# Four tokens per one-hot comparison and 80 candidates per head in the first half of an expert layer

## Chip, cores and metric

The kernel runs on one core of a Trainium2 chip. The metric is the device time of one execution in microseconds (us). Each time below is for the whole program, which is one layer with a token mixer and an expert layer, for 512 tokens of width 2048 in fp32.

## The reference, cut to what matters

The change lies in the expert layer (`peer_ffn`). Each token has 8 heads. Each head scores two sets of 128 sub-keys, takes the 16 best of each, adds them pairwise to 256 candidate sums, and takes the 16 best sums. Each of those names one of 128 x 128 experts, and a softmax over the 16 sums gives the gates.

```python
top_s, top_i = lax.top_k(s, 16)                       # s: [.., 8 heads, 2 halves, 128]
cand_s = (top_s[..., 0, :, None] + top_s[..., 1, None, :]).reshape(B, S, 8, -1)
cand_e = (top_i[..., 0, :, None] * 128 + top_i[..., 1, None, :]).reshape(B, S, 8, -1)
best_s, best_pos = lax.top_k(cand_s, 16)
experts = jnp.take_along_axis(cand_e, best_pos, axis=-1)
gates = softmax(best_s)
act = gelu(einsum('td,tkd->tk', xb, u[experts]))      # u, v: 16384 experts of width 2048
out = einsum('tk,tkd->td', gates * act, v[experts])
```

## The kernel before

The program first runs a token mixer (pooling branch, retention, gates, output projection), then `feed`, `query`, `experts_in` and `experts_out`. The last four are written in a hand-made order: what stands earlier in the code stands earlier in each engine's queue. Every engine works through its queue in that order.

All large matrix products take fp32 data as a high and a low part. `split` (L72 to L74) makes both: ScalarE casts to the high part (L73) and VectorE, or GpSimd where told so, subtracts to get the low part (L74). A weight chunk of 128 x 2048 is converted in two halves of 128 x 1024; `half` hands one out and `convert` makes the next, so that (`converted = 2`) two are kept ready ahead of TensorE. Each half feeds 8 steps of three matrix products (L85 to L87), 24 in all. After each half `tick` runs, which in `experts_in` is `step`, with a counter n from 0 to 255.

`experts_in` computes, for 384 of the tokens, the activation of all 16384 experts (128 blocks of two halves each). After every second half ScalarE applies the gelu to the finished block (L1017, tile `gao`). Beside it, `step` feeds in three side jobs:

- R, `route`: takes the 16 best sums. Per head it adds the 16 x 16 candidates (L837) and runs `top16`: two passes of the 8 largest (L819), two of their positions (L820), one that strikes out the first eight (L822). After the 8 heads it splits positions into row and column (L853, L854), then compares them with 0..15 in 8 steps (L865 to L870) to look up the sub-key numbers. It runs first for the 128 tokens whose experts are gathered, then for three tiles of 128 tokens.
- U, `gathers`: GpSimd issues an indirect DMA for one expert row per token (L929); VectorE multiplies and sums it (L978). Three buffers.
- S, `scatter_gates`: spreads the gates of a tile over a 128 x 128 table per token. For each of 32 groups of four tokens it makes one-hots, multiplies them on TensorE in the next S step (L907), and in the step after that ScalarE copies one part from PSUM (L897) and VectorE adds the other (L898), both into the tile `gsc`. After 16 tokens `gsc` is written to memory (L900). `gsc` has one buffer, so the next copy waits for that write.

The order in `step`: U on even n and on n % 16 == 15; S on odd n once a tile is routed; R on every n until then, later on n % 4 == 1, after S.

The one-hots of one token before: GpSimd compares and scales by the gate's high part (L918), VectorE compares and scales by its low part (L920), ScalarE makes the third with two activations (L922, L923), of which the first takes a per-partition bias. The pool `oh` has 7 buffers, one per token.

From the last two blocks of `query` until the first tile is routed, `low_turns` gives every second low half (L74) to GpSimd. The tables `cos` and `sin` of the mixer lie in a pool that is kept to the end.

Of the kernel before, what the change touches and what calls it, by code (L numbers as in the profile page):

```python
# [17 lines left out]
P = 128  # L18
# [12 lines left out]
POOL_ADA = [1, 1, 1, 1, 2, 2, 2, 2, 2, 2, 0, 0]  # L31
ADA_TURNS = {1: (0,), 2: (1,), 3: (2, 3), 4: (4,), 5: (5,), 6: (6, 7), 7: (8,), 8: (9,), 9: (10, 11), 10: (12,),
             11: (13,), 12: (14,), 13: (15,)}
MAGIC = 12582912.0
TWO_PI = 6.283185307179586476925

# [11 lines left out]
class Mixer:  # L48
# [46 lines left out]

    ahead = 3
    low_engine = None
    low_turns = False
    converted = 1

    def fill(self):
# [12 lines left out]
    def convert(self, eng=None, pair=None):  # L114
        while self.loaded and self.loaded[0][1] is not None:
            self.consume()
        if not self.loaded:
            return
        c = self.loaded[0]
        t, _, s = c  # L120
        h, l = (pair or self.next_pair)()
        if self.low_turns:
            self.low_engine = None if self.low_engine else self.nc.gpsimd
        self.split(t[:, s * 1024:(s + 1) * 1024], h, l, eng or self.low_engine)
        self.ready.append((h, l))
        c[2] += 1
        if c[2] == 2:
            self.loaded.pop(0)
            self.fill()
# [154 lines left out]
    def start(self):  # L284
        nc, a = self.nc, self.a
        stt = nc.vector.scalar_tensor_tensor
        self.cond_scope = ExitStack()
        cp = self.cond_scope.enter_context(self.tc.tile_pool(name="cp", bufs=1))
        with ExitStack() as cs:
            tp = lambda n, b=1: cs.enter_context(self.tc.tile_pool(name=n, bufs=b))  # L290
# [115 lines left out]
    def rotary_tables(self, tmp):  # L406
        nc, a = self.nc, self.a
        ts, stt = nc.vector.tensor_scalar, nc.vector.scalar_tensor_tensor
        self.cos = self.const.tile([P, T], FT, name="cos")
        self.sin = self.const.tile([P, T], FT, name="sin")  # L410
        invf = self.const.tile([P, 1], FT, name="invf")
        nc.gpsimd.dma_start(out=invf, in_=a["inv_freq"])
        pos = tmp.tile([P, T], I32, name="sq")
        nc.gpsimd.dma_start(out=pos, in_=a["positions"].to_broadcast([P, T]))
        yield
        c = _pieces(TWO_PI, (4, 11, 18))
        kk = _pieces(float(65536 - 10430 * np.longdouble("6.283185307179586476925286766559")), (4, 11, 18))
        r, h, n = self.sin, self.cos, tmp.tile([P, T], FT, name="rot", bufs=1)
        ts(out=r, in0=pos, scalar1=1.0, scalar2=None, op0=OP.mult)
        yield  # L420
        ts(out=r, in0=r, scalar1=invf, scalar2=None, op0=OP.mult)
        yield
        ts(out=h, in0=r, scalar1=1.0 / 65536, scalar2=MAGIC, op0=OP.mult, op1=OP.add)
        yield
        ts(out=h, in0=h, scalar1=MAGIC, scalar2=None, op0=OP.subtract)
        yield
        stt(out=r, in0=h, scalar=-65536.0, in1=r, op0=OP.mult, op1=OP.add)
        yield
        stt(out=n, in0=h, scalar=sum(kk), in1=r, op0=OP.mult, op1=OP.add)
        yield  # L430
        ts(out=n, in0=n, scalar1=1.0 / TWO_PI, scalar2=MAGIC, op0=OP.mult, op1=OP.add)
        yield
        ts(out=n, in0=n, scalar1=MAGIC, scalar2=None, op0=OP.subtract)
        yield
        for i in range(4):
            stt(out=r, in0=h, scalar=kk[i], in1=r, op0=OP.mult, op1=OP.add)
            yield
            stt(out=r, in0=n, scalar=-c[i], in1=r, op0=OP.mult, op1=OP.add)
            yield
        ts(out=n, in0=r, scalar1=1.0 / TWO_PI, scalar2=MAGIC, op0=OP.mult, op1=OP.add)  # L440
        yield
        ts(out=n, in0=n, scalar1=MAGIC, scalar2=None, op0=OP.subtract)
        yield
        for v in (c[0] + c[1], c[2] + c[3]):
            stt(out=r, in0=n, scalar=-v, in1=r, op0=OP.mult, op1=OP.add)
            yield
        lim = float(np.nextafter(np.float32(np.pi), np.float32(0)))
        ts(out=r, in0=r, scalar1=lim, scalar2=-lim, op0=OP.min, op1=OP.max)
        yield
        nc.scalar.activation(out=h, in_=r, func=AF.Abs)  # L450
        ts(out=h, in0=h, scalar1=-1.0, scalar2=float(np.pi / 2), op0=OP.mult, op1=OP.add)
        yield
        nc.scalar.activation(out=self.cos, in_=h, func=AF.Sin)
        nc.scalar.activation(out=self.sin, in_=r, func=AF.Sin)
# [110 lines left out]
    def retention(self):  # L565
        nc, a = self.nc, self.a
        self.ret = self.dram.tile([32, P, T], FT, name="ret")
        with ExitStack() as cs:
# [76 lines left out]
                pend = finish  # L645
            self.first_gate = self.gemm_t(self.hn)
            pend()

    def load_pairs(self, src, pool):
        out = []  # L650
# [91 lines left out]
    def query(self):  # L742
# [7 lines left out]
        with ExitStack() as cs:  # L750
# [35 lines left out]
            for j in range(KT):  # L786
                b = first[j] if j < 2 else self.gemm_t(self.fn)
                keep(j, b)
                natural(j)
                if j >= KT - 2:  # L790
                    self.low_turns = True
            self.flush()
        self.extra_scope.close()

# [29 lines left out]
    def route(self, t, pool):  # L824
# [6 lines left out]
        bp = mk([P, H, 16], U32, "bp")  # L831
        v4 = self.tv[t].rearrange("p (h s) r -> p h s r", s=2)
        for h in range(H):
            cand = mk([P, 16, 16], FT, "cand")
            x = v4[:, h, 0, :].unsqueeze(2).broadcast_to([P, 16, 16])
            y = v4[:, h, 1, :].unsqueeze(1).broadcast_to([P, 16, 16])
            tt(out=cand, in0=x, in1=y, op=OP.add)  # L837
            c = cand.rearrange("p a b -> p (a b)")
            self.top16(c, c, bv[:, h, :], bp[:, h, :])
            yield  # L840
        nc.vector.tensor_copy(out=tf, in_=self.ti[t])
# [7 lines left out]
        res = []  # L849
        hi = mk([P, H * 16], U32, "hi")  # L850
        lo = mk([P, H * 16], U32, "lo")
        bpf = bp.rearrange("p h k -> p (h k)")
        nc.vector.tensor_scalar(out=hi, in0=bpf, scalar1=4, scalar2=None, op0=OP.logical_shift_right)  # L853
        nc.vector.tensor_scalar(out=lo, in0=bpf, scalar1=15, scalar2=None, op0=OP.bitwise_and)  # L854
        yield
        f4 = tf.rearrange("p (h s) r -> p h s r", s=2)
        for side, pos in ((0, hi), (1, lo)):
            pf = mk([P, H, 16], FT, f"pf{side}")
            nc.vector.tensor_copy(out=pf.rearrange("p h k -> p (h k)"), in_=pos)
            ix = mk([P, H, 16], FT, f"ix{side}")  # L860
            for q in range(4):
                hs = slice(2 * q, 2 * q + 2)
# [13 lines left out]
    def scatter_gates(self, t, i1, i2, gate, tp, oh, gp):  # L876
# [2 lines left out]
        for i, x in enumerate((i1, i2, gate)):  # L879
            nc.tensor.transpose(out=b[:, i * P:(i + 1) * P], in_=x, identity=self.ident)  # L880
        yield
        tr = tp.tile([P, 4, P], FT, name="tr")
        gh = tp.tile([P, P], FR, name="gh")
        gl = tp.tile([P, P], FT, name="gl")
        nc.scalar.copy(out=tr[:, 0:3, :].rearrange("p a b -> p (a b)"), in_=b[:, 0:3 * P])
        self.split(tr[:, 2, :], gh, gl)
        nc.vector.tensor_scalar(out=tr[:, 3, :], in0=tr[:, 1, :], scalar1=-1.0, scalar2=None, op0=OP.mult)
        yield
        made, summed, gs = [], [], None
        for q in range(P // 4 + 2):  # L890
            for bank, n in summed:
                r = n * 2 % GC
# [6 lines left out]
                if r + 2 == GC:  # L899
                    nc.sync.dma_start(out=self.gd[t * (P // GC) + n * 2 // GC], in_=gs.rearrange("p i t -> p (i t)"))  # L900
            summed = []
            for v in (0, 1):
                if made:
                    bank = self.bank()
                    for u in (0, 1):
                        y, x = made[v * 2 + u]
                        nc.tensor.matmul(bank[:, u * 2 * P:(u + 1) * 2 * P], y, x.rearrange("p h i -> p (h i)"),  # L907
                                         start=True, stop=True)
                    summed.append((bank, 2 * (q - 1) + v))
            made = []  # L910
            if q < P // 4:
                for u in range(4):
                    n = q * 4 + u
                    x = oh.tile([P, 2, P], FR, name="ohx")
                    y = oh.tile([P, P], FR, name="ohy")
                    d = oh.tile([P, P], FT, name="ohd", bufs=2)
                    s = slice(n, n + 1)
                    nc.gpsimd.tensor_scalar(out=x[:, 0, :], in0=self.iota, scalar1=tr[:, 0, s], scalar2=gh[:, s].bitcast(FT),  # L918
                                            op0=OP.is_equal, op1=OP.mult)
                    nc.vector.tensor_scalar(out=x[:, 1, :], in0=self.iota, scalar1=tr[:, 0, s], scalar2=gl[:, s],  # L920
                                            op0=OP.is_equal, op1=OP.mult)
                    nc.scalar.activation(out=d, in_=self.iota, func=AF.Abs, bias=tr[:, 3, s], scale=1.0)  # L922
                    nc.scalar.activation(out=y, in_=d, func=AF.Relu, bias=1.0, scale=-1.0)  # L923
                    made.append((y, x))
            yield

    def gather(self, src, pool, name, k):
# [5 lines left out]
    def experts_in(self):  # L933
# [5 lines left out]
        with ExitStack() as left:  # L939
# [1 line left out]
            lp = lambda n, b=1: left.enter_context(tc.tile_pool(name=n, bufs=b, reuse_waits="tile"))  # L941
            rp_ = lambda n, b=1: right.enter_context(tc.tile_pool(name=n, bufs=b, reuse_waits="tile", side="right"))
            ap, up, gg = lp("ap", 2), lp("up", 3), lp("gg")
            rp, trp, oh, gp = rp_("rp"), rp_("trp"), rp_("oh", 7), rp_("gp")
            act = gg.tile([P, P], FT, name="act")
            gate = gg.tile([P, P], FT, name="ggate")
            fnat = gg.tile([P, D], FT, name="fnat")
# [41 lines left out]
            def step():  # L989
                n = count[0]  # L990
                count[0] += 1
                if scattering:
                    self.low_turns, self.low_engine = False, None
                odd, e = n % 2, n // 2
                if not routed or not scattering:
                    next(R, None)
# [319 lines left out]
```

## Time and profile before

| | |
|---|---|
| median of 3 runs | 4974.7 us (4973.16 to 4975.7) |
| profiled execution, its own time | 4985.34 us |
| span of its instructions | 4983.6 us, 58696 instructions |
| mean granted clock of TensorE | 0.988 of full speed |
| busy: TensorE, weight load, VectorE, ScalarE, GpSimd | 4832.4, 4173.4, 3237.4, 1704.9, 1570.5 us |
| `experts_in`, by its gelu (L1017) | from 2752.8 to 3903.5 us |

The busy times are of one profiled execution. Matrix products are pipelined, so each is shown longer than the step from one to the next; the count of products per microsecond tells better how fast TensorE goes. PE is TensorE, PEld its weight loads, DVE is VectorE, ACT is ScalarE, POOL is GpSimd, SP is the queue that issues most DMAs. An arrow in a row reads "output from inputs".

### The profile page before, as it was taken

To read this page: it belongs to the slowest core of one execution; us is meant where nothing else is said; L and a number is where in the kernel's file an instruction comes from. 1 tells how busy PE (TensorE), PEld (TensorE's weight loads), DVE (VectorE), ACT (ScalarE), POOL (GpSimd) and SP (SyncE) were. 2 spreads that over 40 slices of the span, in tenths; PEclk is the share of its full clock that TensorE was granted. 3 is DMA by queue.
4 is the path that set the end of the run, shared out by engine and by line. 5 is a ranking of instruction groups with operands and counts; after the bars stand their busy time and mean duration, and the time that the engine had idled before them with its cause. 6 is when DMAs were issued, how large, how long until landed. Compare 5 with 4: busy or idle time off the path is not lost.

```text
span 4983.6 us, 58696 instructions
## 1 busy us (share of the span) xinstructions
PE 4832.4 (97%) x22905; PEld 4173.4 (84%) x22905; DVE 3237.4 (65%) x4296; ACT 1704.9 (34%) x2703; POOL 1570.5 (32%) x1125
## 2 busy tenths in 40 slices
PE   6889999999999999999989999999999999999998
PEld 5668888888888888888878999999999888888887
DVE  8873334434332245655567998888787688888876
ACT  3332222222222222222232346556566433332233
POOL 6440000000000010000010367777788344444433
PEclk9999999999999999999999999999999999999999
DMA  6442222222233356765732577887888989898884
GB/s 265 178 148 87 102 102 99 95 102 95 92 126 131 125 190 227 263 228 204 237 107 99 172 275 282 291 295 275 308 294 314 327 310 326 317 332 323 316 284 152
DMA packets 268454, 1058.12 MB, mean 212 GB/s; under 512 B 22656, under 2 KB 73904, under 8 KB 173328
## 3 DMA queue, kind: packets, MB, share of 16 engines
q1 hardware_dynamic: 208960, 726.71, 42.2%
q0 software_dynamic: 54416, 325.48, 17.2%
q8 instruction: 181, 2.97, 0.2%
q10 hardware_dynamic: 4800, 2.16, 0.2%
q14 instruction: 97, 0.79, 0.0%
HBM read 973.53 MB, written 80.75 MB: 212 GB/s over the span
## 4 chain that ended last, share of the span: by engine, by line
PE 72%; DVE 11%; issue 8%; DMA 5%; POOL 2%; ACT 2%; SPq 0%; POOLq 0%; DVEq 0%; ACTq 0%
PE bank L87 24%; PE bank L85 24%; PE bank L86 24%; DVE wlc L74 2%; DVE urow L978 1%; DVE rawc L188 1%; DMA gd<-gsc 1%; DMA rawc<-in_w_ada_dram 1%; POOL ohx L918 1%; DVE u L513 1%; DMA x<-m 1%; ACT whc L73 1%; PE bank L907 1%; DVE gsc L898 0%; DVE eq L869 0%
## 5 line engine op out<-in xcount | busy, mean ns | idle before, releaser
L74 DVE TENSOR_TENSOR wlc<-rawc,whc 128x1024 fp32r<-128x1024 f32 x905 | 1158.3, 1286 | 993.5 <-ACT whc L73 992.9
L73 ACT CAST whc<-rawc 128x1024 fp32r<-128x1024 f32 x968 | 998.9, 1050 | 1995.4 <-PE bank L86 1093.8
L85 PE MATMUL bank<-act,whc 128*128 128x512 f32 x2816 | 1101.8, 391 | 27.8 <-ACT act L347 19.0
L86 PE MATMUL bank<-act,whc 128*128 128x512 f32 x2816 | 1102.8, 392 | 24.1 <-DVE act L356 20.2
L87 PE MATMUL bank<-act,wlc 128*128 128x512 f32 x2816 | 1102.1, 391 | 6.4 <-POOL wlc L74 3.6
L87 PE MATMUL bank<-fh,wlc 128*128 128x384 f32 (+1 forms) x2304 | 792.7, 344 | 15.6 <-DVE wlc L74 12.9
L85 PE MATMUL bank<-fh,whc 128*128 128x384 f32 (+1 forms) x2304 | 793.3, 344 | 4.8 <-ACT whc L73 2.8
L86 PE MATMUL bank<-fl,whc 128*128 128x384 f32 (+1 forms) x2304 | 791.1, 343 | 0.7 <-DVE fl L734 0.5
L86 PEld LDWEIGHTS bank<-act,whc 128*128 128x128 f32 x2816 | 531.8, 189 | 141.0 <-DVE act L356 24.8
L85 PEld LDWEIGHTS bank<-act,whc 128*128 128x128 f32 x2816 | 532.1, 189 | 138.8 <-ACT act L347 19.0
L87 PEld LDWEIGHTS bank<-act,wlc 128*128 128x128 f32 x2816 | 531.8, 189 | 120.3 <-POOL wlc L74 4.9
L918 POOL TENSOR_SCALAR ohx<-iota,tr,gh 128x128 fp32r<-128x128 f32 x384 | 586.9, 1535 | 75.1 <-PE bank L907 70.7
L85 PE MATMUL bank<-whc,ph 128*128 128x512 f32 x1536 | 602.7, 392 | 1.0 <-ACT ph L73 1.0
L87 PE MATMUL bank<-whc,pl 128*128 128x512 f32 x1536 | 600.5, 391 | 0.0
L86 PE MATMUL bank<-wlc,ph 128*128 128x512 f32 x1536 | 597.7, 389 | 1.6 <-DVE wlc L74 1.6
L87 PEld LDWEIGHTS bank<-fh,wlc 128*128 128x128 f32 x2304 | 436.0, 189 | 30.3 <-DVE wlc L74 16.1
L85 PEld LDWEIGHTS bank<-fh,whc 128*128 128x128 f32 x2304 | 436.5, 189 | 15.7 <-ACT whc L73 4.0
L86 PEld LDWEIGHTS bank<-fl,whc 128*128 128x128 f32 x2304 | 436.0, 189 | 11.3 <-DVE fl L734 2.0
L929 POOL DMA_INDIRECT vrow<-in_v_dram,eidx x128 | 273.7, 2138 | 488.4 <-DVE accg L1076 473.2
L188 DVE SCALAR_TENSOR_TENSOR rawc<-rawc,cond 128x2048 f32<-128x2048 f32 x96 | 241.8, 2520 | 198.7 <-DMA rawc<-in_w_ada_dram 198.7
L86 PEld LDWEIGHTS bank<-wlc,ph 128*128 128x128 f32 x1536 | 288.4, 188 | 65.0 <-DVE wlc L74 2.4
L87 PEld LDWEIGHTS bank<-whc,pl 128*128 128x128 f32 x1536 | 288.2, 188 | 64.8 <-DVE pl L74 0.3
(285 smaller groups left out, 5292.9 us busy)
## 6 DMA issues: line engine op xcount, KB each, us to landing
rawc<-in_ut_dram SPq DMA_DIRECT2D x128, 1024.0 KB, 5.7
rawc<-in_v_dram SPq DMA_DIRECT2D x128, 1024.0 KB, 7.5
rawc<-in_w_ada_dram SPq DMA_DIRECT2D x96, 1024.0 KB, 5.3
rawc<-in_w_v_dram SPq DMA_DIRECT2D x32, 1024.0 KB, 4.9
rawc<-in_w_g_dram SPq DMA_DIRECT2D x32, 1024.0 KB, 4.8
rawc<-in_w_br_dram SPq DMA_DIRECT2D x32, 1024.0 KB, 5.0
ga<-gao SPq DMA_DIRECT2D x64, 384.0 KB, 6.8
gd<-gsc SPq DMA_DIRECT2D x24, 1024.0 KB, 10.1
```

Source lines behind the costliest of these rows:

```text
L73: nc.scalar.copy(out=h, in_=src)
L74: (eng or nc.vector).tensor_tensor(out=l, in0=src, in1=h.bitcast(FT), op=OP.subtract)
L85: mm(out, w[0], x[0], start=start, stop=False)
L86: mm(out, w[0], x[1], start=False, stop=False)
L87: mm(out, w[1], x[0], start=False, stop=stop)
L188: nc.vector.scalar_tensor_tensor(out=t, in0=t, scalar=1.0, in1=self.cond, op0=OP.mult, op1=OP.mult, accum_out=self.mod[:, j:j + 1])
L513: nc.vector.tensor_tensor(out=s2[:, PAD:], in0=s[:, PAD:], in1=s[:, PAD - w:PAD + T - w], op=OP.add)
L907: nc.tensor.matmul(bank[:, u * 2 * P:(u + 1) * 2 * P], y, x.rearrange("p h i -> p (h i)"), start=True, stop=True)
L918: nc.gpsimd.tensor_scalar(out=x[:, 0, :], in0=self.iota, scalar1=tr[:, 0, s], scalar2=gh[:, s].bitcast(FT), op0=OP.is_equal, op1=OP.mult)
L929: self.nc.gpsimd.indirect_dma_start(out=t, out_offset=None, in_=src, in_offset=bass.IndirectOffsetOnAxis(ap=self.eidx[:, k:k + 1], axis=0))
L978: nc.vector.scalar_tensor_tensor(out=u, in0=u, scalar=1.0, in1=fnat, op0=OP.mult, op1=OP.mult, accum_out=act[:, i:i + 1])
```

## The change

The one-hots of four tokens are made together: VectorE compares twice (128 x 512 each, the row number and the column number), and ScalarE scales the first comparison by the gate's high and low part, per token: eight multiplications with a per-partition factor. GpSimd's and VectorE's comparisons with scaling and ScalarE's two activations go, and so does the negated copy of the column numbers. `oh` has 2 buffers, each of four tokens.

A head's candidate list has 80 sums instead of 256: rows 0 and 1 with 16 columns, rows 2 and 3 with 8, rows 4 to 7 with 4, rows 8 to 15 with 2. They are added for four heads at a time. Nine small instructions per tile turn a position in the list into row and column.

`low_turns` goes: VectorE makes all low halves there. The pool of `cos` and `sin` is closed after retention.

```diff
+CANDIDATES = ((0, 0, 2, 16), (32, 2, 2, 8), (48, 4, 4, 4), (64, 8, 8, 2))
...
-        if self.low_turns:
-            self.low_engine = None if self.low_engine else self.nc.gpsimd
...
-                if j >= KT - 2:
-                    self.low_turns = True
...
-            cand = mk([P, 16, 16], FT, "cand")
...
-            tt(out=cand, in0=x, in1=y, op=OP.add)
-            c = cand.rearrange("p a b -> p (a b)")
+            if h % 4 == 0:
+                cand = mk([P, 4, 80], FT, "cand")
+                for o, lo, n, w in CANDIDATES:
+                    x = v4[:, h:h + 4, 0, lo:lo + n].unsqueeze(3).broadcast_to([P, 4, n, w])
+                    y = v4[:, h:h + 4, 1, 0:w].unsqueeze(2).broadcast_to([P, 4, n, w])
+                    tt(out=cand[:, :, o:o + n * w].rearrange("p h (a b) -> p h a b", b=w), in0=x, in1=y, op=OP.add)
+            c = cand[:, h % 4, :]
             self.top16(c, c, bv[:, h, :], bp[:, h, :])
...
+        for j, (low, high, by, times) in enumerate(((32, 48, 3, 8), (48, 64, 2, 12), (64, 80, 1, 14))):
+            nc.vector.tensor_scalar(out=lo, in0=bpf, scalar1=low, scalar2=high, op0=OP.max, op1=OP.min)
+            nc.vector.tensor_scalar(out=hi, in0=lo, scalar1=by, scalar2=None, op0=OP.logical_shift_right)
+            nc.vector.scalar_tensor_tensor(out=code, in0=hi, scalar=float(times), in1=code if j else bpf,
+                                           op0=OP.mult, op1=OP.add)
...
             if q < P // 4:
+                x = oh.tile([P, 4, 2, P], FR, name="ohx")
+                y = oh.tile([P, 4, P], FR, name="ohy")
+                d = oh.tile([P, 4, P], FT, name="ohd")
+                s = slice(4 * q, 4 * q + 4)
+                for o, w in ((d, 0), (y, 1)):
+                    nc.vector.tensor_tensor(out=o, in0=iota, in1=tr[:, w, s].unsqueeze(2).broadcast_to([P, 4, P]),
+                                            op=OP.is_equal)
                 for u in range(4):
...
-                    nc.gpsimd.tensor_scalar(out=x[:, 0, :], in0=self.iota, scalar1=tr[:, 0, s], scalar2=gh[:, s].bitcast(FT),
-                                            op0=OP.is_equal, op1=OP.mult)
-                    nc.vector.tensor_scalar(out=x[:, 1, :], in0=self.iota, scalar1=tr[:, 0, s], scalar2=gl[:, s],
-                                            op0=OP.is_equal, op1=OP.mult)
-                    nc.scalar.activation(out=d, in_=self.iota, func=AF.Abs, bias=tr[:, 3, s], scale=1.0)
-                    nc.scalar.activation(out=y, in_=d, func=AF.Relu, bias=1.0, scale=-1.0)
-                    made.append((y, x))
+                    n = slice(4 * q + u, 4 * q + u + 1)
+                    nc.scalar.mul(out=x[:, u, 0, :], in_=d[:, u, :], mul=gh[:, n].bitcast(FT))
+                    nc.scalar.mul(out=x[:, u, 1, :], in_=d[:, u, :], mul=gl[:, n])
+                made.append((x, y))
...
-            rp, trp, oh, gp = rp_("rp"), rp_("trp"), rp_("oh", 7), rp_("gp")
+            rp, trp, oh, gp = rp_("rp"), rp_("trp"), rp_("oh", 2), rp_("gp")
```

## Rows read from the trace of the kernel before

**Rows 1.** The page: TensorE's busy time, and the group of ScalarE's casts.
```profile
PE 4832.4 (97%) x22905; PEld 4173.4 (84%) x22905; DVE 3237.4 (65%) x4296; ACT 1704.9 (34%) x2703; POOL 1570.5 (32%) x1125
...
L73 ACT CAST whc<-rawc 128x1024 fp32r<-128x1024 f32 x968 | 998.9, 1050 | 1995.4 <-PE bank L86 1093.8
```

**Rows 2.** Windows: stretch, length, busy and count by engine, clock, DMA share.
```profile
2850.00:3500.00 650.00, 620.55 (x3570) 615.60 (x3569) 574.01 (x923) 356.90 (x797) 468.67 (x316) 0.98 0.79 282
3500.00:3870.00 370.00, 370.00 (x2181) 369.89 (x2181) 289.78 (x415) 223.73 (x512) 290.50 (x200) 1.00 0.85 303
3040.00:3050.00 10.00, 5.99 (x28) 5.78 (x27) 9.55 (x21) 2.76 (x4) 9.80 (x8) 0.85 0.81 276
```

**Rows 3.** Waits from 2744 to 3905: total us, times, longest.
```profile
ACT gao L1017 <- PE bank L87: 182.3, 32, 13.7
ACT gsc L897 <- DMA gd<-gsc: 153.0, 18, 11.8
...
ACT ohy L923 <- PE bank L907: 129.3, 49, 3.9
...
PE bank L907 <- POOL ohx L918: 14.5, 7, 4.0
PE bank L87 <- DVE wlc L74: 12.9, 10, 5.9
```

**Rows 4.** Groups by shape, 2744 to 3905: busy, mean ns, idle before.
```profile
L918 POOL TENSOR_SCALAR ohx<-iota,tr,gh 128x128 fp32r<-128x128 f32 x384 | 586.9, 1535 | 75.1 <-PE bank L907 70.7
...
L922 ACT ACTIVATE ohd<-iota,tr 128x128 f32<-128x128 f32 x384 | 149.6, 390 | 0.0
L923 ACT ACTIVATE ohy<-ohd 128x128 fp32r<-128x128 f32 x384 | 119.6, 311 | 140.0 <-PE bank L907 129.3
```

**Rows 5.** Groups by shape, 2744 to 2917, VectorE and GpSimd.
```profile
L74 DVE TENSOR_TENSOR wlc<-rawc,whc 128x1024 fp32r<-128x1024 f32 x20 | 30.7, 1540 | 0.0
...
L837 DVE TENSOR_TENSOR cand<-tv 128x256 f32<-128x256 f32 x18 | 18.8, 1044 | 0.2
...
L74 POOL TENSOR_TENSOR wlc<-rawc,whc 128x1024 fp32r<-128x1024 f32 x18 | 47.1, 2617 | 93.1 <-ACT whc L73 93.1
```

**Rows 6.** Single lines: ns min/median/max, first and last start.
```profile
L837 DVE TENSOR_TENSOR cand<-tv x32: 404/420/2627, 2750.9 to 3341.4; 128x256 f32<-128x256 f32 x32
...
L865 DVE TENSOR_TENSOR eq<-pf,iota x32: 677/693/2878, 2790.5 to 3514.4; 128x512 f32<-128x512 f32 x32
...
L819 DVE MAX8 bv<-cand x64: 427/428/430, 2751.3 to 3343.4; 128x8 f32<-128x256 f32 x64
L819 DVE MAX8 tv<-rest x21: 295/295/296, 2700.3 to 2750.2; 128x8 f32<-128x128 f32 x21
```

**Rows 7.** Timeline of VectorE, 2960 to 3000: start us, us, instruction.
```profile
2980.88 1.16 DVE L898 TENSOR_TENSOR gsc<-gsc,bank 128x256 f32<-128x256 f32 x2 [2.50 <-ACT gsc L897]
...
2985.09 1.23 DVE L74 TENSOR_TENSOR wlc<-rawc,whc 128x1024 fp32r<-128x1024 f32 x1 [1.89 <-ACT whc L73]
2986.23 2.29 DVE L978 SCALAR_TENSOR_TENSOR urow<-urow,fnat 128x2048 f32<-128x2048 f32 x1
...
2988.44 1.22 DVE L74 TENSOR_TENSOR wlc<-rawc,whc 128x1024 fp32r<-128x1024 f32 x1
2989.58 1.18 DVE L898 TENSOR_TENSOR gsc<-gsc,bank 128x256 f32<-128x256 f32 x2
2990.66 1.11 DVE L920 TENSOR_SCALAR ohx<-iota,tr,gl 128x128 fp32r<-128x128 f32 x4
```

**Rows 8.** Timeline of ScalarE, 2960 to 3000.
```profile
2980.24 1.08 ACT L897 COPY gsc<-bank 128x256 f32<-128x256 f32 x2 [7.65 <-DMA gd<-gsc]
...
2989.32 0.48 ACT L1017 ACTIVATE gao<-bank 128x384 f32<-128x384 f32 x1
2989.70 1.99 ACT L73 CAST whc<-rawc 128x1024 fp32r<-128x1024 f32 x2
```

**Rows 9.** The chain that ended last, in order of time.
```profile
2969.97 10.17 DMA gd<-gsc
```

More of the change, by code (lines that the diff above doesn't have):

```diff
@@ L97 @@
     low_engine = None
-    low_turns = False
     converted = 1
@@ L286, in start @@
         stt = nc.vector.scalar_tensor_tensor
-        self.cond_scope = ExitStack()
+        self.trig_scope, self.cond_scope = ExitStack(), ExitStack()
+        self.trig = self.trig_scope.enter_context(self.tc.tile_pool(name="trig", bufs=1))
         cp = self.cond_scope.enter_context(self.tc.tile_pool(name="cp", bufs=1))
@@ L408, in rotary_tables @@
         ts, stt = nc.vector.tensor_scalar, nc.vector.scalar_tensor_tensor
-        self.cos = self.const.tile([P, T], FT, name="cos")
-        self.sin = self.const.tile([P, T], FT, name="sin")
+        self.cos = self.trig.tile([P, T], FT, name="cos")
+        self.sin = self.trig.tile([P, T], FT, name="sin")
         invf = self.const.tile([P, 1], FT, name="invf")
@@ L647, in retention @@
             pend()
+        self.trig_scope.close()
     def load_pairs(self, src, pool):
@@ L833, in route @@
         for h in range(H):
-            cand = mk([P, 16, 16], FT, "cand")
-            x = v4[:, h, 0, :].unsqueeze(2).broadcast_to([P, 16, 16])
-            y = v4[:, h, 1, :].unsqueeze(1).broadcast_to([P, 16, 16])
-            tt(out=cand, in0=x, in1=y, op=OP.add)
-            c = cand.rearrange("p a b -> p (a b)")
+            if h % 4 == 0:
[5 more added lines that the diff above has]
+            c = cand[:, h % 4, :]
             self.top16(c, c, bv[:, h, :], bp[:, h, :])
@@ L851, in route @@
         lo = mk([P, H * 16], U32, "lo")
+        code = mk([P, H * 16], U32, "code")
         bpf = bp.rearrange("p h k -> p (h k)")
-        nc.vector.tensor_scalar(out=hi, in0=bpf, scalar1=4, scalar2=None, op0=OP.logical_shift_right)
-        nc.vector.tensor_scalar(out=lo, in0=bpf, scalar1=15, scalar2=None, op0=OP.bitwise_and)
+        for j, (low, high, by, times) in enumerate(((32, 48, 3, 8), (48, 64, 2, 12), (64, 80, 1, 14))):
[3 more added lines that the diff above has]
+                                           op0=OP.mult, op1=OP.add)
+        nc.vector.tensor_scalar(out=hi, in0=code, scalar1=4, scalar2=None, op0=OP.logical_shift_right)
+        nc.vector.tensor_scalar(out=lo, in0=code, scalar1=15, scalar2=None, op0=OP.bitwise_and)
         yield
@@ L858, in route @@
             pf = mk([P, H, 16], FT, f"pf{side}")
-            nc.vector.tensor_copy(out=pf.rearrange("p h k -> p (h k)"), in_=pos)
+            nc.vector.tensor_scalar(out=pf.rearrange("p h k -> p (h k)"), in0=pos, scalar1=0.0 if side else 39.0,
+                                    scalar2=None, op0=OP.subtract)
             ix = mk([P, H, 16], FT, f"ix{side}")
@@ L881, in scatter_gates @@
         yield
-        tr = tp.tile([P, 4, P], FT, name="tr")
+        tr = tp.tile([P, 3, P], FT, name="tr")
         gh = tp.tile([P, P], FR, name="gh")
         gl = tp.tile([P, P], FT, name="gl")
-        nc.scalar.copy(out=tr[:, 0:3, :].rearrange("p a b -> p (a b)"), in_=b[:, 0:3 * P])
+        nc.scalar.copy(out=tr.rearrange("p a b -> p (a b)"), in_=b[:, 0:3 * P])
         self.split(tr[:, 2, :], gh, gl)
-        nc.vector.tensor_scalar(out=tr[:, 3, :], in0=tr[:, 1, :], scalar1=-1.0, scalar2=None, op0=OP.mult)
         yield
         made, summed, gs = [], [], None
+        iota = self.iota.unsqueeze(1).broadcast_to([P, 4, P])
         for q in range(P // 4 + 2):
@@ L901, in scatter_gates @@
             summed = []
-            for v in (0, 1):
-                if made:
+            if made:
+                x, y = made.pop()
+                for v in (0, 1):
                     bank = self.bank()
                     for u in (0, 1):
-                        y, x = made[v * 2 + u]
-                        nc.tensor.matmul(bank[:, u * 2 * P:(u + 1) * 2 * P], y, x.rearrange("p h i -> p (h i)"),
-                                         start=True, stop=True)
+                        nc.tensor.matmul(bank[:, u * 2 * P:(u + 1) * 2 * P], y[:, 2 * v + u, :],
+                                         x[:, 2 * v + u, :, :].rearrange("p h i -> p (h i)"), start=True, stop=True)
@@ L909, in scatter_gates @@
                     summed.append((bank, 2 * (q - 1) + v))
-            made = []
             if q < P // 4:
-                for u in range(4):
[L913 to L917, printed above, removed]
-                    nc.gpsimd.tensor_scalar(out=x[:, 0, :], in0=self.iota, scalar1=tr[:, 0, s], scalar2=gh[:, s].bitcast(FT),
-                                            op0=OP.is_equal, op1=OP.mult)
-                    nc.vector.tensor_scalar(out=x[:, 1, :], in0=self.iota, scalar1=tr[:, 0, s], scalar2=gl[:, s],
-                                            op0=OP.is_equal, op1=OP.mult)
-                    nc.scalar.activation(out=d, in_=self.iota, func=AF.Abs, bias=tr[:, 3, s], scale=1.0)
-                    nc.scalar.activation(out=y, in_=d, func=AF.Relu, bias=1.0, scale=-1.0)
-                    made.append((y, x))
+                x = oh.tile([P, 4, 2, P], FR, name="ohx")
@@ L991, in step @@
                 count[0] += 1
-                if scattering:
-                    self.low_turns, self.low_engine = False, None
                 odd, e = n % 2, n // 2
```

## Prediction

> **What bounds the kernel now.** The page is read first: TensorE is busy for 97% of the span [rows 1]. So a change elsewhere counts only through the time in which it makes TensorE wait. The table of windows comes second, and in it the count of products, not the busy time. From 3500 to 3870 TensorE gets through 2181 products in 370 us, 5.895 per us, with nothing lost. From 2850 to 3500 it gets through 3570 in 650 us, which at that pace would be 605.6 us [rows 2]. **So 44 us are lost in `experts_in`**, all before 3500, and this is all that the change can win there. For a pair of steps n (48 products and 4 for the one-hots) the free pace is 52 / 5.895 = 8.82 us.
>
> The waits come third. TensorE waited 14.5 us for GpSimd's one-hots and 12.9 us for low halves from VectorE [rows 3]; the rest of the 44 us is the slower clock behind a wait (0.85 in the slice from 3040, with 28 products in 10 us) and many small gaps [rows 2]. GpSimd's comparison takes 1535 ns on average [rows 4], four per pair; beside its low halves, VectorE's subtraction takes 1540 ns and the candidate sum 1044 ns [rows 5], where the sum's median is 420 [rows 6]. The two engines hold each other up.
>
> The timelines come last, for the order of the queues. VectorE, from 2985.09: low half, expert row (U), low half, two sums into `gsc`, one-hots [rows 7]. ScalarE: two `gsc` copies, one-hots, gelu, two casts [rows 8]. **To be seen here:** apart from the write of `gsc`, nothing that ScalarE does in this loop waits for VectorE. ScalarE waits for TensorE (182.3 us at the gelu, 129.3 at the one-hots) and for the write of `gsc` (153.0) [rows 3]. So its casts are early, and VectorE always finds them.
>
> **What goes.** GpSimd's 384 comparisons and 18 low halves go [rows 4, 5], and with them both waits on GpSimd and the blocking of VectorE. The one-hot buffers were 7 single tokens, so the fourth token of a step waited for the product just issued (129.3 us on ScalarE [rows 3]); two buffers of four wait for a product one step older, so this goes too. GpSimd's queue keeps the gathers, which are no longer behind comparisons. I let the whole 44 us be returned: **-44 us**.
>
> **Before the first tile is routed.** VectorE takes back 18 low halves at 1.14 us from start to start [rows 7]: +20.5 us. It is no longer blocked: (1.540 - 1.222) x 20 + (1.044 - 0.420) x 18 = -17.6 us, with 1.22 us as the free subtraction [rows 5, 6, 7]. A largest-eight pass takes 428 ns over 256 columns and 295 over 128 [rows 6], 1.04 ns a column, so over 80 it is 183 ns shorter; five such passes a head give -0.92 us, and four sums for four heads instead of one per head give some -0.1. For 16 heads that is -16 us. Nine decode instructions a tile at no more than 0.3 us (the 128-column pass) give +2.7 us, twice. Net -8 us on VectorE, so the gaps there should close; this is inside the 44 us. If it isn't true, some 10 of the 44 stay.
>
> **During the scatter: a new loop.** ScalarE's eight scalings read what VectorE has just compared. In VectorE's queue that comparison stands behind low half, row, low half and sums; in ScalarE's queue the gelu and the next cast stand behind the scalings; and VectorE's next low half needs that cast. So in each pair of steps the work goes once round both engines, nothing of it overlapped:
>
> - VectorE: low half 1.14, row 2.21, low half 1.14, two sums 1.08, each from start to start [rows 7]
> - first comparison, 128 x 512: 0.69, as L865, which has the same size and kind [rows 6]
> - eight scalings of 128 x 128. The trace has none; the nearest row is the activation with a per-partition operand, 390 ns [rows 4]. Two casts of 1.05 us run in 1.99 [rows 1, 8], so neighbours overlap by 0.10: 8 x 0.29 = 2.32
> - gelu 0.38 from start to start, then the cast 1.05 [rows 1, 8]
>
> The sum is 10.01 us, against TensorE's 8.82. The second comparison (0.6) and R run on VectorE while ScalarE scales, so the shorter lists win nothing here: R must last over 2.32 + 0.38 + 1.05 - 0.6 = 3.1 us to count, and a head should take under 2.
>
> Two additions. U comes a second time on n % 16 == 15, one pair in eight: 2.21 / 8 = 0.28. The write of `gsc` ends one group of four pairs: from its start at 2969.97, 10.17 us long [rows 9], to VectorE's next sum at 2980.88 [rows 7] are 10.91 us, while the loop would be back after 10.01 - 1.08 = 8.93; so 1.98 / 4 = 0.50. **A pair takes 10.79 us, 1.97 more than TensorE needs.** The 96 pairs with one-hots: 96 x 1.97 = +189 us.
>
> Off this: each of three tiles starts with two halves ready ahead, 2 x 24 / 5.895 = 8.1 us that TensorE can use up, and has four pairs without one-hots in which the lead is won back: -24. The first two steps of each tile have no sums: 6 x 1.08 = -6.5. **+158 us.**
>
> **What costs nothing.** The nine decode instructions of the later tiles lie in R, under the scalings. The closed pool of `cos` and `sin` issues nothing, and the mixer's order stays; were its start or end to shift, the price should be a wait like those of the rows, under 10 us. No DMA is added or moved; SP's queue is as before.
>
> **Sum:** -44 + 158 = +114 us. The profiled execution took 4985.34 us, 10.6 more than the median of the runs, so the difference is put on the median: 4974.7 + 114 = 5089, **about 5090 us**.
>
> **Bounds.** A scaling costs at least what an activation without per-partition operand does, 0.311 - 0.10 = 0.21 [rows 4], and at most 0.39 with no overlap: 2.32 becomes 1.68 or 3.12, or -61 and +77 us. Without any wait on the `gsc` write: -48 at most, but its row shows it. I take the middle of the scalings, since their operand is of the kind of the 390 ns row.
>
> **Rivals.** *Faster: the loop doesn't close.* ScalarE stays far enough ahead that its scalings never hold back a cast; TensorE then has its free pace and the 44 us come back: 4930 us. VectorE's load would allow this: 2 x 1.14 + 1.125 x 2.21 + 1.08 + 2 x 0.6 + about 1 for half a step of R = 8.05 us a pair, under 8.82. The Trainium skill, "SBUF — State Buffer", section "Who interferes with whom", has a rule that would make this the result: a VectorE instruction with two inputs in SBUF and a GpSimd instruction that reads SBUF lock each other out for a whole instruction. By that rule the change removes the contention, since the gathers are all that GpSimd keeps, and the time would be 4930; the trace agrees that there is blocking (median 420, longest 2627 ns for the candidate sum), but the loop comes out of other rows. It decides where a pair closes in under 8.82 us, and even with scalings of 0.21 it is 10.15. Against it stands the order of both queues in the timelines. Chance 0.10.
>
> *Slower still: the clock.* TensorE now idles 2 us a pair, some 4 us where `gsc` is written. Behind a 4 us wait the slice from 3040 had 28 products at a clock of 0.85: 59 - 28 products are 5.3 us, 1.3 more than the wait. 24 such places: +30 us, 5120. Chance 0.15.
>
> *The loop is there but cheap:* scalings of 0.21 give 5090 - 61 = 5029 us. Chance 0.15. *Nothing to be seen:* loop and winnings cancel; this needs 114 / 96 = 1.2 us less a pair than the sum. Chance 0.03.
>
> **How the numbers follow.** The forecast as summed has a chance of 0.57. A measurement of this kernel tells about 0.2%, 10 us, from no change. Faster by more: 0.10, the first rival. Same: 0.03. Slower: 0.57 + 0.15 + 0.15 = 0.87. The range leaves out the two rivals below and a few far ends: from the cheap scalings with a little less wait on `gsc`, 5015, to the dear ones, 5090 + 77 = 5167, so 5170.
>
> **What would show it.** In the profile after: the count of products per us from 2920 on falls from 5.9 to about 4.8, evenly and not in single gaps; the largest waits are ScalarE's scalings for VectorE's comparison and VectorE's low half for ScalarE's cast, and ScalarE's waits for TensorE at the gelu are nearly gone; a scaling lasts about 390 ns; starts of the gelu on odd steps lie some 10 us apart. `experts_in` ends about 114 us later, and the rest of the kernel is as long as before. Wrong it would be if the gelu still waits for TensorE in most pairs.

## The result and the profile after

The changed kernel takes 5120.5 us (median of 4 runs, 5117.78 to 5122.9) against 4975.2 us: ratio 1.029, 95% interval 1.0272 to 1.0308. It is slower, as forecast, by 145 us where 115 was said; 5120.5 lies in the range of 5015 to 5170. The two profiled executions differ by less, 5116.5 - 4983.6 = 132.9 us of span, because that of before (4985.34) was 10.1 us above its median and that of after (5118.27) 2.2 us below. The steps of the sum are compared with this 132.9.

All of it lies in `experts_in`. Its gelu (now L1021) starts at 2752.8 in both and ends at 4036.1 instead of 3903.5; behind it are 1080.4 us, before 1080.1. The windows of the kernel after (stretch, length, TensorE, weight load, VectorE, ScalarE, GpSimd busy and count, clock, DMA share):

```profile
2752.00:2920.00 168.00, 166.98 (x962) 166.39 (x961) 141.76 (x335) 56.32 (x76) 21.45 (x14) 1.00 0.63 229
2920.00:4000.00 1080.00, 993.07 (x5326) 943.71 (x5325) 772.19 (x1042) 565.33 (x1268) 180.66 (x115) 0.96 0.68 254
```

Read the counts. Ahead of the first tile 962 products run in 168 us, 5.73 per us, where the kernel before had

```profile
2752.00:2920.00 168.00, 156.61 (x886) 154.65 (x885) 162.40 (x285) 51.22 (x65) 65.29 (x33) 0.98 0.59 203
```

886: 76 products, 13 us, are won there, and VectorE is busy for 142 us instead of 162. From 2920 on TensorE gets through 4.93 per us instead of 5.5 to 5.9 [rows 2]. VectorE's busy share is lower than before too (772 of 1080 us), and GpSimd's is a sixth. Nobody is overloaded; all wait. The waits of the kernel after, from 2744 to 4050 (total us, times, longest):

```profile
ACT ohx L928 <- DVE ohd L924: 374.4, 95, 6.7
DVE wlc L76 <- ACT whc L75: 299.0, 115, 6.0
...
ACT gao L1021 <- PE bank L89: 150.5, 27, 7.3
ACT gsc L905 <- DMA gd<-gsc: 79.5, 17, 5.5
PEld bank L89 <- DVE wlc L76: 66.8, 70, 1.6
PEld bank L87 <- ACT whc L75: 46.3, 65, 2.0
PE bank L89 <- DVE wlc L76: 44.0, 68, 1.2
```

The first two lines are the loop: ScalarE waits for VectorE's comparison 95 times (3.9 us each), VectorE for ScalarE's cast 115 times (2.6 us). GpSimd's comparisons, which TensorE waited for, and ScalarE's waits for a free one-hot buffer [rows 3] are gone, and some 70 small waits of TensorE for low halves have come. The timeline shows one turn, first VectorE (start us, us, instruction, idle before it):

```profile
3067.66 1.23 DVE L76 TENSOR_TENSOR wlc<-rawc,whc 128x1024 fp32r<-128x1024 f32 x1 [3.29 <-ACT whc L75]
3068.81 2.28 DVE L984 SCALAR_TENSOR_TENSOR urow<-urow,fnat 128x2048 f32<-128x2048 f32 x1
...
3071.02 1.22 DVE L76 TENSOR_TENSOR wlc<-rawc,whc 128x1024 fp32r<-128x1024 f32 x1
3072.16 1.13 DVE L906 TENSOR_TENSOR gsc<-gsc,bank 128x256 f32<-128x256 f32 x2
3073.19 0.69 DVE L924 TENSOR_TENSOR ohd<-iota,tr 128x512 f32<-128x512 f32 x1
...
3076.18 0.69 DVE L878 TENSOR_REDUCE ix<-eq 128x32 f32<-128x512 f32 x1
3077.78 1.23 DVE L76 TENSOR_TENSOR wlc<-rawc,whc 128x1024 fp32r<-128x1024 f32 x1 [0.92 <-ACT whc L75]
```

then ScalarE:

```profile
3073.98 0.41 ACT L928 ACTIVATE ohx<-ohd,gh 128x128 fp32r<-128x128 f32 x1 [4.42 <-DVE ohd L924]
3074.29 0.39 ACT L929 ACTIVATE ohx<-ohd,gl 128x128 fp32r<-128x128 f32 x1
...
3076.34 0.46 ACT L1021 ACTIVATE gao<-bank 128x384 f32<-128x384 f32 x1
3076.71 1.98 ACT L75 CAST whc<-rawc 128x1024 fp32r<-128x1024 f32 x2
```

From one low half behind a cast (3067.66) to the next (3077.78) it is 10.12 us, against 10.01 in the sum. To be seen: VectorE's second comparison and a whole step of R (its last instruction is L878) end before the cast does (VectorE still idles 0.92), so a shorter R wins nothing here.

### The profile page after: what moved, and what is told of

It is laid out like the page before. It is cut to its first block, busy times and chain, and to the rows that moved or that the text cites. A ratio compares the mean times of both kernels' runs of the same rounds, so it can differ in the third digit from the quotient of the medians.

```text
span 5116.5 us, 58002 instructions
## 1 busy us (share of the span) xinstructions
PE 4908.3 (96%) x22905; PEld 4203.2 (82%) x22905; DVE 3192.0 (62%) x4156; ACT 1716.0 (34%) x2703; POOL 983.8 (19%) x722
## 4 chain that ended last, share of the span: by engine, by line
PE 62%; DVE 13%; issue 10%; DMA 9%; ACT 6%; POOL 1%; DVEq 0%; ACTq 0%; SPq 0%; POOLq 0%
PE bank L89 20%; PE bank L87 20%; PE bank L88 20%; DMA gd<-gsc 4%; DMA rawc<-in_w_ada_dram 3%; DVE urow L984 3%; DVE wlc L76 2%; DVE gsc L906 2%; ACT whc L75 2%; ACT ohx L928 1%; ACT ohx L929 1%; DVE rawc L187 1%; DMA x<-m 1%; DVE ohd L924 1%; DMA rawc<-in_v_dram 1%
## 5 line engine op out<-in xcount | busy, mean ns | idle before, releaser
L89 PE MATMUL bank<-fh,wlc 128*128 128x384 f32 (+1 forms) x2304 | 811.4, 352 | 45.2 <-DVE wlc L76 44.0
L87 PE MATMUL bank<-fh,whc 128*128 128x384 f32 (+1 forms) x2304 | 812.0, 352 | 36.4 <-ACT whc L75 30.5
L88 PE MATMUL bank<-fl,whc 128*128 128x384 f32 (+1 forms) x2304 | 802.2, 348 | 0.6 <-DVE fl L735 0.5
L88 PEld LDWEIGHTS bank<-fl,whc 128*128 128x128 f32 x2304 | 445.1, 193 | 11.3 <-DVE fl L735 1.9
L935 POOL DMA_INDIRECT urow<-in_u_dram,eidx x128 | 202.1, 1579 | 1220.7 <-DVE urow L984 953.5
```

The source lines that it names most:

```text
L87: mm(out, w[0], x[0], start=start, stop=False)
L88: mm(out, w[0], x[1], start=False, stop=False)
L89: mm(out, w[1], x[0], start=False, stop=stop)
L935: self.nc.gpsimd.indirect_dma_start(out=t, out_offset=None, in_=src, in_offset=bass.IndirectOffsetOnAxis(ap=self.eidx[:, k:k + 1], axis=0))
```

## The experiments

**1. The loop opened.** The scalings (and the column comparison that goes with them) are issued one S step later.

```diff
+            if compared:
+                d = compared.pop()
...
+                    nc.scalar.mul(out=x[:, u, 0, :], in_=d[:, u, :], mul=gh[:, n].bitcast(FT))
+                    nc.scalar.mul(out=x[:, u, 1, :], in_=d[:, u, :], mul=gl[:, n])
+                made.append((x, y))
             if q < P // 4:
...
+                compared.append(d)
```

> The changed kernel, but each group's eight scalings and its column comparison are issued one S step later than its row comparison, so ScalarE reads a comparison that VectorE made a pair of steps earlier; the same instructions otherwise (one S step more per tile, and one pause before it less). Loop theory (VectorE comparison, ScalarE scalings, cast, VectorE low half): the loop is open, TensorE goes back to about 5.9 products per us and the 44 us of before come back too: 4930 to 4950 us, ScalarE's wait for the row comparison under 30 us in total (374 in the changed kernel). Load theory (the work that went from GpSimd to VectorE and ScalarE is what costs): the work is the same, so 5110 to 5125 us.

Measured: 4974.43 us, 0.9997 of before (0.9987 to 1.0007). All of the 145 us are gone, and ScalarE's wait for the comparison is 29.9 us instead of 374.4, with the same work; so the load theory is out. But it is not 4930 to 4950: some 35 us stay lost (measured against experiment 7 below), and in the waits of this kernel, from 2744 to 3900, one stands out:

```profile
ACT gsc L904 <- DMA gd<-gsc: 163.5, 17, 11.7
DVE wlc L76 <- ACT whc L75: 108.6, 61, 6.0
DVE gsc L905 <- ACT gsc L904: 91.8, 23, 9.6
```

The copies wait for the write of `gsc`, with the casts behind them: experiment 7 takes this up.

**2 and 3. Four more scalings, inside the loop and outside.** Both add the same ScalarE work into a tile that nobody reads: behind the eight scalings and reading the comparison, or at the head of the step and reading a constant.

```diff
+                junk = oh.tile([P, P], FT, name="ohj", bufs=1)
+                for u in range(4):
+                    nc.scalar.mul(out=junk, in_=d[:, u, :], mul=gl[:, 4 * q + u:4 * q + u + 1])
```

> The changed kernel with four more scalings of 128 x 128 per group behind the eight, reading the same comparison and writing a tile that nobody reads (the result is untouched). Loop theory: each lengthens the loop by its 0.29 us from start to start: 96 x 4 x 0.29 = +111 us, 5220 to 5240 us. Load theory: ScalarE is busy for some 55% of the stretch, so 1.2 us more per pair fit into its idle time: 5120 to 5135 us.

> The changed kernel with the same four additional scalings per group, but issued at the head of the S step, ahead of the copies from PSUM, and reading the constant row of numbers instead of the comparison (the result is untouched). Loop theory: they fall into the some 4 us per pair in which ScalarE waits for the comparison, so nothing: 5115 to 5130 us. Load theory: the same as with the four behind the comparison, whatever that gives.

Measured: 5237.84 us inside, 5115.56 outside. The same 384 instructions cost 117 us at one place and nothing at the other. That is the strongest evidence: not how much ScalarE does counts, but what stands between VectorE's comparison and the next cast.

That 117 lies so near the 111 that were said is in part luck. Inside the loop the four, which write one tile, take 1.59 us up to the gelu, some 0.4 each and not 0.29, so a plain turn goes from 10.11 to 11.64 us:

```profile
3157.34 1.69 ACT L932 ACTIVATE ohj<-ohd,gl 128x128 f32<-128x128 f32 x4
3158.93 0.47 ACT L1024 ACTIVATE gao<-bank 128x384 f32<-128x384 f32 x1
...
3170.57 0.47 ACT L1024 ACTIVATE gao<-bank 128x384 f32<-128x384 f32 x1
```

The pairs behind a write of `gsc`, on the other hand, take 11.7 to 11.9 us in most cases, as in the changed kernel (11.7 to 12.0): there the longer turn takes the place of part of the wait.

**4. Lists and low halves only.** The one-hots of before in the changed kernel (the code of `scatter_gates` and its 7 buffers as before).

> The changed kernel with the one-hots of before (GpSimd, VectorE and ScalarE, 7 buffers); short lists, decode, all low halves on VectorE and the closed pool stay. Loop theory: no loop, so no loss; the gap of about 13 us ahead of the first tile stays closed, GpSimd's late one-hots stay: 4945 to 4965 us. If lists, decode or the low halves on VectorE cost something by themselves: over 4975 us.

Measured: 4957.73 us, ratio 0.9961 (0.9947 to 0.9975). The other half of the change, by itself, is a gain of some 20 us: 13 ahead of the first tile as in the changed kernel; the rest lies in the scatter (from 2920 to 3500 3303 products, where the kernel before has 3240). I put it down to VectorE's shorter R, but no run shows that alone, and it hangs on the write of `gsc`: without the wait for it (experiment 7) this half of the change has 3394 products there against 3388, next to nothing.

**5. The other half alone.** The new one-hots with lists, decode and low halves of before.

> The new one-hots alone: candidate lists of 256 and GpSimd's every second low half ahead of the first tile are as before. Loop theory: R is still hidden behind scalings, gelu and cast (0.6 + 2.96 us for the longest step of R against 2.32 + 0.38 + 1.05), so the long lists cost nothing during the scatter; the gap of some 13 us ahead of the first tile comes back: 5128 to 5140 us. Load theory: 24 heads at 1 us more on VectorE on top: over 5150 us.

Measured: 5128.13 us, 8 more than the changed kernel. From 2850 to 2920 it has 350 products where the changed kernel has 397; from 2920 to 3500 it has 2869, the changed kernel 2855. So in the loop 256 candidates cost no more than 80.

**6. Comparison ahead of the sums.** The same instructions, with both comparisons moved up in front of the copies and sums.

```diff
         for q in range(P // 4 + 2):
+            if q < P // 4:
...
+                for o, w in ((d, 0), (y_, 1)):
+                    nc.vector.tensor_tensor(out=o, in0=iota, in1=tr[:, w, s].unsqueeze(2).broadcast_to([P, 4, P]),
+                                            op=OP.is_equal)
             for bank, n in summed:
```

> The changed kernel with both comparisons issued ahead of the copies and sums into gsc instead of behind them; the same instructions in another order. Loop theory: the two sums (1.08 us) leave the loop, but the scalings now stand behind copies that wait for the write of gsc, which costs some 4 us once in four pairs: 10.25 instead of 10.8 us a pair, some -55 us: 5050 to 5080 us. Load theory: order changes nothing, 5110 to 5125 us.

Measured: 5043.08 us, -77 us and more than expected. The starts of the gelu, from the timelines of ScalarE, show the loop's length. The changed kernel:

```profile
3164.28 0.47 ACT L1021 ACTIVATE gao<-bank 128x384 f32<-128x384 f32 x1
...
3174.39 0.47 ACT L1021 ACTIVATE gao<-bank 128x384 f32<-128x384 f32 x1
...
3184.51 0.47 ACT L1021 ACTIVATE gao<-bank 128x384 f32<-128x384 f32 x1
```

the kernel with the comparison first:

```profile
3125.29 0.47 ACT L1023 ACTIVATE gao<-bank 128x384 f32<-128x384 f32 x1
...
3133.69 1.07 ACT L913 COPY gsc<-bank 128x256 f32<-128x256 f32 x2 [6.05 <-DMA gd<-gsc]
3136.88 0.47 ACT L1023 ACTIVATE gao<-bank 128x384 f32<-128x384 f32 x1
3145.94 0.47 ACT L1023 ACTIVATE gao<-bank 128x384 f32<-128x384 f32 x1
...
3155.06 0.47 ACT L1023 ACTIVATE gao<-bank 128x384 f32<-128x384 f32 x1
...
3164.14 0.47 ACT L1023 ACTIVATE gao<-bank 128x384 f32<-128x384 f32 x1
...
3173.46 1.10 ACT L913 COPY gsc<-bank 128x256 f32<-128x256 f32 x2 [6.96 <-DMA gd<-gsc]
3176.64 0.47 ACT L1023 ACTIVATE gao<-bank 128x384 f32<-128x384 f32 x1
```

10.1 us has become 9.1: the two sums of 1.08 us have left the loop, to a tenth. Where the write of `gsc` ends the wait, most pairs take 11.2 to 11.6 us, as the first one shown (11.59), and a few 12.2 to 12.7, as the last one (12.50). So the write costs 2.1 to 2.5 us in most cases and 3.4 or a little more in a few, less than the 4 that were expected, and the gain is larger.

**7. Without the wait for the write of `gsc`.** Copies and sums are made for two steps at once, so that the write has two pairs of steps. It is put into the changed kernel, into experiment 1, into experiment 4 and into the kernel before.

```diff
-            for bank, n in summed:
+            for bank, n in summed if len(summed) == 4 else ():
...
-            summed = []
+            summed = [] if len(summed) == 4 else summed
```

> The changed kernel, but copies and sums into gsc are made for two steps at once in every second step (four banks instead of two), so that the write of gsc, one step in four before, has two pairs of steps before the next copy. The same instructions and bytes. The loop stays; only its wait for the write, summed at 0.5 us a pair, goes: -35 to -50 us, 5070 to 5085 us. If that wait is no part of the path: 5115 to 5125 us.

> The kernel with the scalings one step later, and with the sums into gsc for two steps at once. If what was left there over the free pace of TensorE was the wait for the write of gsc (163.5 us on ScalarE, 11.7 at most): 4935 to 4955 us, faster than both kernels. If it was VectorE's load: 4970 to 4980 us.

> The kernel with the one-hots of before, short lists and all low halves on VectorE, and with the sums into gsc for two steps at once. It has lost some 20 us to waits: if most of these come from the write of gsc, 4935 to 4947 us; if from GpSimd's late one-hots, 4950 to 4960 us as without it.

> The kernel before, with only the sums into gsc made for two steps at once. If the three losses of before add up (some 13 us ahead of the first tile, the write of gsc, GpSimd's late one-hots), only the write's goes, some 13 us as with the one-hots of before and short lists: 4960 to 4968 us. If the change's parts were worth nothing beside it: 4940 to 4950 us.

Measured: in the changed kernel 5084.15 us, -36, at the upper end of what was said (the sum had 0.50 x 96 = 48). In the kernel before 4956.1 us, ratio 0.9953 (0.9936 to 0.9969), some 20 us where 8 to 16 were expected: the single buffer cost more there than I thought. With the one-hots of before and short lists 4944.64 us, 0.9933 (0.992 to 0.9947), as said for the case that the write cost most there. With the scalings later **4938.83 us, 0.9922 (0.9909 to 0.9936)**: the fastest of all, faster than both kernels. Its windows:

```profile
2920.00:3500.00 580.00, 580.00 (x3419) 579.97 (x3418) 516.13 (x746) 364.74 (x829) 118.50 (x74) 1.00 0.83 304
3500.00:3850.00 350.00, 350.00 (x2060) 349.96 (x2059) 263.21 (x300) 201.22 (x448) 68.52 (x45) 1.00 0.82 296
```

TensorE runs through at 5.89 products per us, the free pace. What was left of experiment 1 was the write, not VectorE's load, which at 516 of 580 us is higher than in the changed kernel (431 in the same stretch).

The kernel before with the sums by two also shows what its waits for GpSimd were. TensorE's wait for GpSimd's one-hots, and GpSimd's comparisons:

```profile
PE bank L907 <- POOL ohx L918: 0.4, 1, 0.4
...
L918 POOL TENSOR_SCALAR ohx<-iota,tr,gh 128x128 fp32r<-128x128 f32 x384 | 632.5, 1653 | 36.2 <-PE bank L907 32.0
```

The comparisons are no faster than in the kernel before (1653 ns on average against 1535 [rows 4]), yet TensorE waits 0.4 us for them instead of 14.5 [rows 3], and from 2920 to 3500 it gets through 3388 products instead of 3240, some 25 us more. So most of what the kernel before lost in the scatter hung on the write of `gsc`. By which steps that wait made the one-hots late was not followed.

## Why the prediction was right, and where it was off

**Right: the loop.** That the scalings join two queues into a loop of about 10 us, longer than TensorE's 8.82, is what made the forecast, and the trace and experiments 1, 2, 3 and 6 show it. The terms held: comparison 0.69 (measured mean 0.684), a scaling 390 ns (391 and 387) and 0.29 from start to start, R hidden (experiment 5). The mean of the 96 pairs, by the starts of the gelu, is 10.82 us; 10.79 was said. More than half of them take 10.1, those with a second U 12.3, those behind the write of `gsc` mostly 11.7 to 12.

**Right as a size, off in its cause: the 44 us.** The free pace was read rightly: experiment 7 runs at it, 4938.83, 39 us under the 4977.5 of the kernel before beside it (47 us less span in the profiled executions). The first 13 of the 44 us are in the windows ahead of the first tile. But "What goes" gives the rest to GpSimd's comparisons and the one-hot buffers, and the runs do not show that: the kernel before wins some 20 us with these left as they are, once it need not wait for the write of `gsc` (experiment 7), and experiment 1, in which they are gone and the write is still waited for, is no faster than the kernel before. The forecast does not suffer, because the wait for the write stands in the sum of the loop. The reading behind it was too strong: that, apart from the write, nothing on ScalarE waits for VectorE, and that VectorE always finds its casts. Rows 7 have a wait of 1.89 us for a cast, and the waits of the kernel before, from 2744 to 3905, have these too:

```profile
DVE wlc L74 <- ACT whc L73: 92.3, 50, 6.0
...
ACT gate L845 <- DVE gate L844: 21.5, 4, 9.8
ACT coef L982 <- DVE urow L978: 19.4, 4, 6.5
```

**Off: sizes, 19 us in the profiled executions.** My sum left out two other jobs of ScalarE. The softmax's exponential stands ahead of the gelu with two loads of tables, 3.0 us more (two pairs, 13.1 us); the gelu of every 32 gathered rows waits for VectorE's last row (three pairs that have a second U as well, 12.0 to 13.6 us instead of 12.3):

```profile
3052.58 1.28 ACT L846 ACT_TABLE_LOAD   x1
3053.87 0.31 ACT L846 ACTIVATE gate<-gate 128x128 f32<-128x128 f32 x1
3054.20 1.28 ACT L1021 ACT_TABLE_LOAD   x1
...
3123.57 0.23 ACT L988 ACTIVATE coef<-act 128x32 f32<-128x32 f32 x1 [3.50 <-DVE urow L984]
```

The plain turn is 10.11 and not 10.01. Against this the write costs less than the 48 us in the sum: experiment 7 wins 36 in the changed kernel, and in the lengths the pairs behind a write come to some 37 us over plain ones. So that 10.79 lies so close to 10.82 is partly luck. Two pairs a tile, without sums, take 9.0 to 9.5 (one, with a second U, 11.3), as I had said; they are already in the 10.82. So 96 pairs cost 96 x (10.82 - 8.82) = 192 us, where I had 189 - 6.5 = 182.5. And the lead at the start of a tile, set at 24 us, saves about 16: behind the last pair of each tile the next two take 11.0 to 11.4 us together, where the free pace has 16.7; and 192 - 44 - 133 leaves 15.

The other 12 us of the miss come mostly from the step that put the difference on the median. The 44 us were read from an execution that took 4985.34. On that one the sum gives 4985.34 + 114 = 5099, and the free pace 4941, close to the 4938.83 of experiment 7.

**The rivals.** "Faster, the loop doesn't close": it closes. But its price was right, 4930 against the 4938.83 of experiment 7, once the write of `gsc` is out of the way as well; I had not said that it must be. (Most of the 8 us between is the step with the median again.) The rule of the Trainium skill that stood beside it ("SBUF — State Buffer", section "Who interferes with whom") agrees with the trace as far as it goes: with GpSimd's comparisons and low halves gone, the candidate sum and its neighbours no longer show durations of 2 to 3 us, and L873, the comparison in R, takes 711 ns at most where rows 6 have up to 2878. But that blocking cost little time in the scatter, as the 1653 ns in experiment 7 show; the queues decided, and the rule says nothing on them. "Slower still, the clock": the granted clock did fall, to 0.96 from 2920 to 4000, and to 0.83 in some slices of 20 us, but a plain turn stays at 10.1 us, the sum of ScalarE's and VectorE's own durations, so the clock costs nothing that the lengths show. That the price of this rival, 5120, is the measured time is chance: it put 1.3 us on each pair behind a write, and those are no longer than the sum had them without it (mostly 11.7 to 12.0, said 10.01 + 1.98). No run changed the clock by itself. "Cheap": scalings of 0.21 were not seen.

**Of the signs** the count was said as 4.8 and is 4.93. ScalarE's waits for TensorE at the gelu did not nearly vanish in the total (150.5 us, 27 times, before 182.3, 32 times [rows 3]): most lie ahead of the first tile, where there is no loop (103.5 us to 2925, then 32.3 us, 6 times, to 3990). I should have given that sign for the scatter alone.

## What to carry to other kernels

Before moving work between engines, write down each engine's queue for one turn of the loop and look whether a new dependence joins two queues into a circle; the length of that circle, not any engine's load, is then the pace, and work that is off the circle is free as long as it fits into the waits. A circle of this kind is opened by issuing the consumer one turn later than its producer, with no work saved: 145 us here. And where one wait is removed and the gain is smaller than its price, look for the next one of the same kind, here a single buffer that waits for its own write.

## What was not expected of the hardware

The regularity: apart from the pairs with an additional row, a write, the softmax or the gelu of rows, and the pairs next to these, the loop keeps 10.1 us to within 0.1 over hundreds of us, and moving 1.08 us of sums out of it gives 9.1. Durations and start-to-start distances taken from a trace in which these instructions never stood in this order (and one of them did not exist) added up to 1%. And the single buffer for `gsc`, which looked hidden in the kernel before because TensorE hardly ever waited for it directly, was worth some 20 us there.
